# Split weight halves of two FFNs: two separate buffer rings, or one fixed turn of seven over both

## The chip, the cores and the metric

The kernel runs on one core of a Trainium2 chip. The metric is the device time of one execution in microseconds (us), a median over several runs; a lower time is better. A profile of one execution says which engine did what at which time of its span. The engines named here are PE (matrix multiplication), ACT (ScalarE), DVE (VectorE), POOL (GpSimd) and SP (which issues most of the DMAs).

## The reference, cut to what matters

One layer of an encoder is computed for 256 rows of width 2048, in 32-bit floats. The change touches the two half-FFNs, the first and the third stage of the layer:

```python
D_MODEL = 2048
SEQ = 256
D_FF = ((8 * D_MODEL // 3 + 255) // 256) * 256       # 5632

def swiglu(h, w_gate, w_up, w_down):
    return (jax.nn.silu(h @ w_gate) * (h @ w_up)) @ w_down

for i in range(DEPTH):                                # DEPTH = 1
    x = x + 0.5 * swiglu(rms_norm(x, ffn1_norm[i]), ffn1_w_gate[i], ffn1_w_up[i], ffn1_w_down[i])
    ...   # input projection, S5 state-space heads, stick-breaking attention, output projection
    x = x + 0.5 * swiglu(rms_norm(x, ffn2_norm[i]), ffn2_w_gate[i], ffn2_w_up[i], ffn2_w_down[i])
    ...   # per-layer embedding
```

## The kernel before, in words

**Split operands.** Each matrix product is built from rounded parts. A weight tile, 128 x 1024 in 32-bit floats (two blocks of 512 columns), is split into an upper part `hi`, a rounded copy that ACT makes (line 181), and a lower part `lo = src - hi`, which DVE makes (line 184). The activations are split in the same way. PE then adds up three products: hi x hi, lo x hi (both read the weight's upper part) and hi x lo (which reads its lower part). A pair of tiles, one `hi` and one `lo`, is called a half here, since a loaded weight tile `raw` of 128 x 4 x 512 (1 MB) gives two of them.

**Columns and chunks.** The up and gate products of an FFN run over eleven blocks f of 512 columns, the down products over two pairs of such blocks. Part of each block is computed in the plain way: `Seven.column` loads a `raw`, and each of its halves feeds twelve matmuls of 512 columns (`gemm_half`, lines 305, 306 and 310). The rest is computed by `Seven.chunk`, a scheme of the Strassen kind: from two `raw` tiles it forms seven products instead of eight. Three of the seven take a half of a `raw` as it is (products 1, 2, 3), four take a sum of such halves, which DVE adds first (`Seven.add`, line 487; products 5, 6, 4, 7). Each product splits its operand and feeds six matmuls (lines 480, 481, 483). The sums form a chain: t1 feeds product 5, t2 = t1 + ... product 6, t4 = t2 + ... product 4; t3 stands by itself.

**Where chunks are used.** FFN 1 computes its blocks f = 0 to 6 in the plain way, since a preparation for the S5 stage occupies the storage (`early = 7`). At f = 7 that preparation is closed, a pool `sums1` is opened in its storage, DVE forms the sums of activations (`whole_rows`, line 426, and `sum_forms`, line 441), and the chunks begin. FFN 2 has its pool `sums2` from its beginning. At the end of each block f, DVE adds the last product bank (line 606), multiplies (line 608) and turns blocks (`turn_blocks`, line 216).

**The two rings.** A plain half takes its two tiles from the pool `wp` under the tags `whi` and `wlo`, four buffers each. A summed half takes them from the pool of the phase under the tags `shi` and `slo`, three buffers each:

```python
hi, lo = (
    (self.pool if own else wp).tile([P, 2, NB], F32R, tag=s, name=uid(s), bufs=3 if own else None)
    for s in (("shi", "slo") if own else ("whi", "wlo"))
)
```

A half can be split as soon as its ring has a free buffer, that is, when PE has done with the half that used it. The tag `raw` has five buffers, each given back when DVE has done with both halves of it. In the down products two of the five hold x.

**What sets the order.** The program is recorded line by line; a scheduler then orders each engine's instructions before the run, by the recorded order and by when it reckons that operands and buffers are there. On the chip each engine takes its instructions in that order. `step()` runs side work (turns, transfers, norms) that has been put off by so many halves.

Of the kernel before, what the change touches and what calls it, by code (L numbers as in the profile page):

```python
# [2 lines left out]

# [7 lines left out]
F32R = mybir.dt.float32r  # L11
# [5 lines left out]
P = 128  # L17
# [9 lines left out]
NB = 512  # L27
# [6 lines left out]
def layer_kernel(ctx: ExitStack, tc: tile.TileContext, a: dict, shapes: dict, out: bass.AP):  # L34
# [18 lines left out]
    wp = ctx.enter_context(tc.tile_pool(name="wts", bufs=4))  # L53
# [9 lines left out]
    def uid(s):  # L63
        count[0] += 1
        return f"{s}_{count[0]}"
# [7 lines left out]
    def phase(name):  # L73
        return tc.tile_pool(name=name, bufs=1, reuse_waits="tile")
# [175 lines left out]
    def first_quarters(w, xn):  # L250
# [28 lines left out]
        xn.parted(1, second.rearrange("p (j s) -> p j s", j=4))  # L279
        return [(h, *parts[h]) for h in range(2)], weight_split(raws[1], 4)  # L280

    def weight_split(raw, nk, own=None):
        for h in range(nk // 2):
            if own:
                hi, lo = (own.tile([P, 2, NB], F32R, name=uid(s)) for s in ("whi", "wlo"))
            else:
                hi, lo = (wp.tile([P, 2, NB], F32R, tag=s, name=uid(s)) for s in ("whi", "wlo"))
            split(hi, lo, raw[:, 2 * h : 2 * h + 2, :])
            yield h, hi, lo

# [155 lines left out]
    class Seven:  # L446
# [20 lines left out]
            self.begun.add(z)  # L467
            return fresh

        def product(self, z, left, src, own, final):  # L470
            hi, lo = (
                (self.pool if own else wp).tile([P, 2, NB], F32R, tag=s, name=uid(s), bufs=3 if own else None)
                for s in (("shi", "slo") if own else ("whi", "wlo"))
            )
            split(hi, lo, src)
            ps = self.bank(z)
            begin = self.begin(z)
            lh, ll = left
            for j in range(2):
                nc.tensor.matmul(ps, lhsT=lh[j], rhs=hi[:, j], start=begin and j == 0, stop=False)  # L480
                nc.tensor.matmul(ps, lhsT=ll[j], rhs=hi[:, j], start=False, stop=False)  # L481
            for j in range(2):
                nc.tensor.matmul(ps, lhsT=lh[j], rhs=lo[:, j], start=False, stop=z in final and j == 1)  # L483
# [6 lines left out]
        def chunk(self, kb, final=()):  # L490

            raws = []
            for w, n0 in self.ws:
                raw = wp.tile([P, 4, NB], F32, tag="raw", name=uid("raw"), bufs=5)
                nc.sync.dma_start(
                    raw, w[4 * kb * P : 4 * (kb + 1) * P, n0 : n0 + NB].rearrange("(j p) n -> p j n", p=P)
                )
                raws.append(raw)
            b11, b21, b12, b22 = (raw[:, 2 * h : 2 * h + 2, :] for raw in raws for h in range(2))
            parts, sums = self.act(kb), self.sums(kb)  # L500

            def whole(k, t):
                return [[u[:, 2 * k + j, t * P : (t + 1) * P] for j in range(2)] for u in parts]

            def summed(z):
                return [[u[:, z, j * P : (j + 1) * P] for j in range(2)] for u in sums]

            self.product(1, whole(0, 0), b11, False, final)
            t1 = self.add(b11, b12)
            self.product(5, summed(0), t1, True, final)  # L510
            step()
            t2 = self.add(t1, b22)
            self.product(6, summed(1), t2, True, final)
            t4 = self.add(t2, b21)
            self.product(4, whole(1, 1), t4, True, final)
            step()
            t3 = self.add(b12, b22)
            self.product(7, summed(2), t3, True, final)
            self.product(2, whole(1, 0), b21, False, final)
            step()  # L520
            self.product(3, summed(3), b22, False, final)
            step()

        def column(self, side, kbs, final=False):
# [14 lines left out]
    def ffn(i, xn, nxt, bg=None):  # L539
        wg, wu, wd = (a[f"ffn{i}_w_{s}"][0] for s in ("gate", "up", "down"))  # L540
        hT = []
        pools = ExitStack()
        early = 7 if bg else 0
        sevens = None if bg else pools.enter_context(phase(f"sums{i}"))
        hp = pools.enter_context(phase(f"h{i}"))
        side = ExitStack()
        prep = bg(side) if bg else None
# [15 lines left out]
        for f in range(NF):  # L563
            if prep and f == early:
                finish(prep)
                side.close()
                prep = None
                sevens = pools.enter_context(phase(f"sums{i}"))
                hp = pools.enter_context(phase(f"h{i}b"))
                sums = [sum_forms(sevens, whole_rows(sevens, xn(kb)), "h") for kb in range(2)]  # L570
            if sevens and f:
                sg, hh = com("sg"), com("h")
                gate_cols, up_cols = ([u[:, t * NB : (t + 1) * NB] for t in range(TT)] for u in (sg, hh))

                def opened(s, g=gate_cols, u=up_cols):
                    nc.scalar.copy(g[0], s.bank(1))
                    nc.vector.tensor_tensor(out=u[0], in0=s.bank(6), in1=g[0], op=ALU.add)
                    nc.vector.tensor_tensor(out=u[1], in0=s.bank(7), in1=u[0], op=ALU.add)

                def gated(s, g=gate_cols, u=up_cols, hh=hh):  # L580
                    for z, (ps, other) in enumerate(((s.bank(2), g[0]), (s.bank(4), u[1]))):
                        nc.vector.tensor_tensor(out=g[z], in0=ps, in1=other, op=ALU.add)
                        nc.scalar.activation(g[z], g[z], AF.Silu, scale=xn.rs(z))
                    v = hh.rearrange("p (t n) -> p t n", t=TT)
                    nc.vector.tensor_tensor(
                        out=v, in0=s.bank(5).unsqueeze(1).to_broadcast([P, TT, NB]), in1=v, op=ALU.subtract
                    )

                s = Seven(xn, lambda kb: sums[kb], ((wg, f * NB), (wu, f * NB)), sevens)
                two = f % 2 == (0 if bg else 1)  # L590
                if f == early:
                    s.column(0, (1, 2, 3))
                    s.chunk(0, (*shared, 2, 4))
                    put_off(0, opened, s)
                elif two:
                    s.chunk(0)
                    s.column(0, (2, 3))
                    s.chunk(1, (*shared, 2, 4))
                    put_off(0, opened, s)
                else:  # L600
                    s.chunk(0, shared)
                    put_off(0, opened, s)
                    s.column(0, (1, 2, 3), True)
                put_off(0, gated, s)
                s.column(1, (2, 3) if two and f != early else (1, 2, 3), True)
                nc.vector.tensor_tensor(out=hh, in0=s.banks[3.8], in1=hh, op=ALU.add)
                for t in range(TT):
                    nc.vector.scalar_tensor_tensor(
                        out=up_cols[t], in0=up_cols[t], scalar=xn.rs(t), in1=gate_cols[t], op0=ALU.mult, op1=ALU.mult
                    )  # L610
                put_off(2, turned, hp, f, hh)
                continue

            def gate():
                for t in range(TT):
                    nc.scalar.activation(sg[:, t * NB : (t + 1) * NB], pg[t], AF.Silu, scale=xn.rs(t))

            first = ()
            if f == 0 and bg:
                warm_up(10)  # L620
                first = first_quarters(wg, xn)
            if f == 0 and not bg:
                both = gemm_pair(xn, ((wg, 0), (wu, 0)), KD)
                pg = next(both)
                sums = [sum_forms(sevens, whole_rows(sevens, xn(kb))) for kb in range(2)]
            else:
                pg = gemm_block(xn, wg, f * NB, KD, first)
            sg = com("sg")
            if f == 0 and bg:
                for n in range(ND):  # L630
                    put_off(n, load_x, n)
                    put_off(n + 2, xn.squares, n)
                put_off(6, gate)
            else:
                gate()
            pu = gemm_block(xn, wu, f * NB, KD) if f or bg else next(both)
            if prep and f == 0:
                start(prep)
            hh = com("h")
            for t in range(TT):  # L640
                nc.vector.scalar_tensor_tensor(
                    out=hh[:, t * NB : (t + 1) * NB], in0=pu[t], scalar=xn.rs(t),
                    in1=sg[:, t * NB : (t + 1) * NB], op0=ALU.mult, op1=ALU.mult,
                )
            put_off(2, turned, hp, f, hh)
# [31 lines left out]
        for n in range(0, ND, 2):  # L677
# [16 lines left out]
            left = sum(u[0] == "s" for u in plan)  # L694
            for u in plan:
                kb, final = int(u[1:]), u == plan[-1]
# [965 lines left out]
```

## Time and profile before

| | us |
|---|---|
| median of 3 runs | 1852.45 |
| lowest and highest of them | 1851.65 and 1853.28 |
| time of the profiled execution | 1852.7 |
| its span, from the first to the last instruction | 1850.6 |
| PE busy in the span | 1838.3 |
| DVE busy | 1460.6 |
| ACT busy | 1027.4 |

The time of the profiled execution is 2.1 us more than its span; what lies around the span belongs to the start and the end of an execution. Lines such as L184 are lines of the kernel before. In the profile a group of instructions is named by its output and inputs, without buffer numbers: `wlo<-raw,whi` is the lower part of a plain half, `slo<-sum,shi` that of a summed one. In the trace of the changed kernel a plain half may be called `shi` and a summed one `whi`.

### The profile page before, as it was taken

What the parts mean: (1) busy time and instruction counts of PE and PEld (TensorE: products, weight loads), DVE (VectorE), ACT (ScalarE), POOL (GpSimd) and SP (SyncE); (2) the same over time, 40 slices, a digit from 0 to 9 for tenths busy, and PEclk for the clock granted to TensorE, in tenths of its full rate; (3) what the DMA queues carried; (4) which work ended last, traced back from release to release, by engine and by line L of the source; (5) the groups of instructions that cost most, each with busy time, mean ns of one, the idle gap of its engine ahead of it and who ended that gap; (6) DMA issues with size and microseconds to landing.
All of it is one profiled execution on the core that took longest, in us unless ns stands there. A gap on an engine that the chain in (4) does not pass through costs nothing.

```text
span 1850.6 us, 23946 instructions
## 1 busy us (share of the span) xinstructions
PE 1838.3 (99%) x9032; PEld 1518.5 (82%) x9032; DVE 1460.6 (79%) x1718; ACT 1027.4 (56%) x1187; POOL 63.3 (3%) x108
## 2 busy tenths in 40 slices
PE   9999999999999999999999999999999999999998
PEld 7888888778888888888897888888888888888887
DVE  8967665998888876687567798989898978887665
ACT  7444443655564656365685565655555555565654
POOL 0011000000000000010021000000000000000000
PEclk9999999999999999999999999999999999999999
DMA  9888868566756567675646776665656675666663
GB/s 334 281 274 277 252 217 246 173 228 200 241 196 213 192 217 248 190 262 166 216 142 218 224 262 216 235 206 198 218 198 219 207 244 185 223 195 217 208 219 125
DMA packets 232307, 406.36 MB, mean 220 GB/s; under 512 B 26784, under 2 KB 50720, under 8 KB 231904
## 3 DMA queue, kind: packets, MB, share of 16 engines
q1 hardware_dynamic: 227824, 392.81, 63.8%
q0 software_dynamic: 3648, 10.62, 1.8%
q8 instruction: 70, 1.15, 0.2%
q10 hardware_dynamic: 720, 1.41, 0.2%
q14 instruction: 45, 0.37, 0.1%
HBM read 373.46 MB, written 11.93 MB: 208 GB/s over the span
## 4 chain that ended last, share of the span: by engine, by line
PE 92%; DVE 3%; DMA 2%; ACT 2%; SPq 1%; issue 1%; DVEq 0%; ACTq 0%
PE acc L305 18%; PE acc L310 18%; PE acc L306 18%; PE aux L305 7%; PE aux L306 7%; PE aux L310 7%; PE acc L480 3%; PE acc L481 2%; PE acc L483 2%; PE aux L480 2%; PE aux L483 2%; PE aux L481 2%; DVE wlo L184 1%; SPq L1170 1%; DMA raw<-in_w_in 1%
## 5 line engine op out<-in xcount | busy, mean ns | idle before, releaser
L181 ACT CAST whi<-raw 128x1024 fp32r<-128x1024 f32 x639 | 668.1, 1052 | 684.8 <-PE acc L306 388.9
L184 DVE TENSOR_TENSOR wlo<-raw,whi 128x1024 fp32r<-128x1024 f32 x639 | 772.0, 1221 | 297.9 <-ACT whi L181 295.1
L305 PE MATMUL acc<-whi,nhi 128*128 128x512 f32 x1232 | 482.9, 392 | 1.8 <-ACT whi L181 1.7
L306 PE MATMUL acc<-whi,nlo 128*128 128x512 f32 x1232 | 479.9, 390 | 0.0
L310 PE MATMUL acc<-wlo,nhi 128*128 128x512 f32 x1232 | 340.6, 389 | 0.2 <-DVE wlo L184 0.2
L305 PEld LDWEIGHTS acc<-whi,nhi 128*128 128x128 f32 x1232 | 231.5, 188 | 52.2 <-ACT whi L181 3.0
L310 PEld LDWEIGHTS acc<-wlo,nhi 128*128 128x128 f32 x1232 | 231.2, 188 | 48.8 <-DVE wlo L184 0.6
L306 PEld LDWEIGHTS acc<-whi,nlo 128*128 128x128 f32 x1232 | 231.6, 188 | 47.2
L306 PE MATMUL acc<-whi,hlo 128*128 128x512 f32 x376 | 146.4, 389 | 0.0
L305 PE MATMUL acc<-whi,hhi 128*128 128x512 f32 x376 | 146.3, 389 | 0.0
L181 ACT CAST shi<-sum 128x1024 fp32r<-128x1024 f32 x108 | 113.4, 1052 | 43.1 <-DVE sum L487 39.6
L306 PE MATMUL aux<-whi,hlo 128*128 128x512 f32 x344 | 133.8, 389 | 0.0
L305 PE MATMUL aux<-whi,hhi 128*128 128x512 f32 x344 | 133.8, 389 | 0.0
L184 DVE TENSOR_TENSOR slo<-sum,shi 128x1024 fp32r<-128x1024 f32 x108 | 130.9, 1216 | 0.6 <-ACT shi L181 0.5
L310 PE MATMUL acc<-wlo,hhi 128*128 128x512 f32 x376 | 114.6, 389 | 0.2 <-DVE wlo L184 0.2
L310 PE MATMUL aux<-wlo,hhi 128*128 128x512 f32 x344 | 106.0, 389 | 0.0
L306 PE MATMUL aux<-whi,nlo 128*128 128x512 f32 x240 | 93.4, 389 | 0.0
L305 PE MATMUL aux<-whi,nhi 128*128 128x512 f32 x240 | 93.4, 389 | 0.0
L306 PEld LDWEIGHTS acc<-whi,hlo 128*128 128x128 f32 x376 | 70.6, 188 | 15.1 <-DVE hlo L184 0.4
L310 PEld LDWEIGHTS acc<-wlo,hhi 128*128 128x128 f32 x376 | 70.5, 188 | 15.2 <-DVE wlo L184 0.6
L305 PEld LDWEIGHTS acc<-whi,hhi 128*128 128x128 f32 x376 | 70.6, 188 | 14.6
L306 PEld LDWEIGHTS aux<-whi,hlo 128*128 128x128 f32 x344 | 64.6, 188 | 13.5
(345 smaller groups left out, 2162.6 us busy)
## 6 DMA issues: line engine op xcount, KB each, us to landing
raw<-in_ffn_w_up SPq DMA_DIRECT2D x88, 1024.0 KB, 5.8
raw<-in_ffn_w_down SPq DMA_DIRECT2D x88, 1024.0 KB, 5.1
raw<-in_ffn_w_gate SPq DMA_DIRECT2D x86, 1024.0 KB, 6.2
raw<-in_w_in SPq DMA_DIRECT2D x32, 1024.0 KB, 5.7
raw<-in_w_out SPq DMA_DIRECT2D x16, 1024.0 KB, 5.3
raw<-in_w_ple_gate SPq DMA_DIRECT2D x16, 1024.0 KB, 5.1
hT<-mid SPq DMA_DIRECT2D x160, 64.0 KB, 3.5
h<-mid SPq DMA_DIRECT2D x176, 32.0 KB, 3.6
```

Of the source, the lines that this page charges most:

```text
L181: copy = nc.scalar.copy(hi, src)
L184: nc.vector.tensor_tensor(out=lo, in0=src, in1=hi.bitcast(F32), op=ALU.subtract)
L305: nc.tensor.matmul(ps[t], lhsT=lh, rhs=hi[:, j, cols], start=start and j == 0, stop=False)
L306: nc.tensor.matmul(ps[t], lhsT=ll, rhs=hi[:, j, cols], start=False, stop=False)
L310: nc.tensor.matmul(ps[t], lhsT=lh, rhs=lo[:, j, cols], start=False, stop=stop and j == 1)
L480: nc.tensor.matmul(ps, lhsT=lh[j], rhs=hi[:, j], start=begin and j == 0, stop=False)
L481: nc.tensor.matmul(ps, lhsT=ll[j], rhs=hi[:, j], start=False, stop=False)
L483: nc.tensor.matmul(ps, lhsT=lh[j], rhs=lo[:, j], start=False, stop=z in final and j == 1)
L1170: nc.sync.dma_start(zt[0][p1 : p1 + HC, z], sv[p0 : p0 + HC, r % 2 * 2 + r // 2])
```

## The change

The change gives each half of an FFN with chunks, plain or summed, its buffers by one counter. While a pool of sums is open, the halves are numbered i = 0, 1, 2, ... in the order in which the program is recorded; those with i modulo 7 equal to 1, 3 or 5 take `shi` and `slo` of the pool of sums, the other four take `whi` and `wlo` of `wp`. The number of buffers stays four and three. Outside of these phases all halves take `wp`, as before. The tiles' contents and the matmuls are the same. `Seven.product` no longer has an argument `own`.

```diff
+    ring = [None, 0]
+
+    def weight_pair():
+
+        extra, i = ring
+        ring[1] += 1
+        pool, tags = (extra, ("shi", "slo")) if extra and i % 7 % 2 else (wp, ("whi", "wlo"))
+        return [
+            pool.tile([P, 2, NB], F32R, tag=s, name=uid(s), bufs=3 if pool is extra else None) for s in tags
+        ]
+
+    @contextmanager
+    def sums_phase(name):
+        with phase(name) as pool:
+            ring[:] = [pool, 0]
+            yield pool
+            ring[0] = None
+
     def weight_split(raw, nk, own=None):
         for h in range(nk // 2):
             if own:
                 hi, lo = (own.tile([P, 2, NB], F32R, name=uid(s)) for s in ("whi", "wlo"))
             else:
-                hi, lo = (wp.tile([P, 2, NB], F32R, tag=s, name=uid(s)) for s in ("whi", "wlo"))
+                hi, lo = weight_pair()
             split(hi, lo, raw[:, 2 * h : 2 * h + 2, :])
             yield h, hi, lo
...
-        def product(self, z, left, src, own, final):
-            hi, lo = (
-                (self.pool if own else wp).tile([P, 2, NB], F32R, tag=s, name=uid(s), bufs=3 if own else None)
-                for s in (("shi", "slo") if own else ("whi", "wlo"))
-            )
+        def product(self, z, left, src, final):
+            hi, lo = weight_pair()
             split(hi, lo, src)
...
-            self.product(1, whole(0, 0), b11, False, final)
+            self.product(1, whole(0, 0), b11, final)
             t1 = self.add(b11, b12)
-            self.product(5, summed(0), t1, True, final)
+            self.product(5, summed(0), t1, final)
             step()
...
-        sevens = None if bg else pools.enter_context(phase(f"sums{i}"))
+        sevens = None if bg else pools.enter_context(sums_phase(f"sums{i}"))
...
-                sevens = pools.enter_context(phase(f"sums{i}"))
+                sevens = pools.enter_context(sums_phase(f"sums{i}"))
```

The scheduler orders the changed program anew. On PE the order stays that of the products as they are recorded, with some matmuls of neighbouring products exchanged; on ACT and DVE, the two engines that split, many halves move by a few places against each other, and a few loads move on SP. POOL's order is the same.

More of the change, by code (lines that the diff above doesn't have):

```diff
@@ L1 @@
 import math
-from contextlib import ExitStack
+from contextlib import ExitStack, contextmanager
 import concourse.bass as bass
@@ L506, in summed @@
                 return [[u[:, z, j * P : (j + 1) * P] for j in range(2)] for u in sums]
-            self.product(1, whole(0, 0), b11, False, final)
+            self.product(1, whole(0, 0), b11, final)
             t1 = self.add(b11, b12)
-            self.product(5, summed(0), t1, True, final)
+            self.product(5, summed(0), t1, final)
             step()
             t2 = self.add(t1, b22)
-            self.product(6, summed(1), t2, True, final)
+            self.product(6, summed(1), t2, final)
             t4 = self.add(t2, b21)
-            self.product(4, whole(1, 1), t4, True, final)
+            self.product(4, whole(1, 1), t4, final)
             step()
             t3 = self.add(b12, b22)
-            self.product(7, summed(2), t3, True, final)
-            self.product(2, whole(1, 0), b21, False, final)
+            self.product(7, summed(2), t3, final)
+            self.product(2, whole(1, 0), b21, final)
             step()
-            self.product(3, summed(3), b22, False, final)
+            self.product(3, summed(3), b22, final)
             step()
```

## The prediction

> **What bounds the kernel now.** I read the page first, then the stretches of the span by engine, then PE's waits, and last the timelines of PE and DVE where PE waits.
>
> ```profile
> span 1850.6 us, 23946 instructions
> PE 1838.3 (99%) x9032; PEld 1518.5 (82%) x9032; DVE 1460.6 (79%) x1718; ACT 1027.4 (56%) x1187; POOL 63.3 (3%) x108
> ```
>
> PE is the bound: 12.3 us of the span are not PE's. The change leaves every matmul as it is, so all that it can give or take are idle times of PE in the FFN stages. The stretches show where these are (PE, PEld, DVE, ACT, POOL busy with counts, then granted clock, DMA share, GB/s):
>
> ```profile
> 376.00:420.00 44.00, 42.33 (x185) 34.47 (x184) 43.07 (x43) 25.97 (x27) 0.00 (x0) 1.00 0.71 234
> 420.00:600.00 180.00, 180.00 (x793) 148.70 (x792) 152.38 (x152) 100.22 (x102) 4.40 (x8) 1.00 0.63 212
> 1090.00:1380.00 290.00, 290.00 (x1276) 239.03 (x1274) 265.04 (x257) 160.73 (x166) 0.00 (x0) 1.00 0.65 214
> ```
>
> From 420 to 600 us (FFN 1) and from 1090 to 1380 us (FFN 2) PE never idles. There the change can only lose. In the first chunks of FFN 1 DVE is full (43.07 of 44 us) and PE loses. The waits say to whom:
>
> ```profile
> ACT whi L181 <- PE acc L306: 388.9, 272, 3.0
> PE acc L480 <- ACT shi L181: 2.6, 2, 1.7
> PE aux L480 <- ACT shi L181: 0.9, 1, 0.9
> PE acc L310 <- DVE wlo L184: 0.3, 2, 0.2
> ```
>
> The first row is the ring's price to ACT: 388.9 us of waiting for a buffer that PE still reads. It costs PE nothing, since PE's own waits for halves are 2.6, 0.9 and 0.3 us, and they name summed halves or a lower part. The places, with the steady pace ahead of them:
>
> ```profile
> 319.69 0.39 PE L306 MATMUL acc<-whi,nlo 128*128 128x512 f32 x1
> 319.92 0.61 PE L310 MATMUL acc<-wlo,nhi 128*128 128x512 f32 x2
> ...
> 337.80 0.50 PE L480 MATMUL aux<-shi,hhi 128*128 128x512 f32 x1 [0.89 <-ACT shi L181]
> 338.15 0.39 PE L481 MATMUL aux<-shi,hlo 128*128 128x512 f32 x1
> ...
> 366.04 0.50 PE L480 MATMUL acc<-shi,nhi 128*128 128x512 f32 x1 [0.97 <-ACT shi L181]
> ...
> 409.56 0.50 PE L480 MATMUL acc<-shi,nhi 128*128 128x512 f32 x1 [1.67 <-ACT shi L181]
> ...
> 632.72 0.40 PE L481 MATMUL aux<-shi,nlo 128*128 128x512 f32 x1
> 633.26 0.50 PE L483 MATMUL aux<-slo,nhi 128*128 128x512 f32 x1
> ...
> 648.44 0.40 PE L306 MATMUL acc<-whi,hlo 128*128 128x512 f32 x1
> 649.01 0.50 PE L310 MATMUL acc<-wlo,hhi 128*128 128x512 f32 x1 [0.18 <-DVE wlo L184]
> ```
>
> A matmul follows the one before it after 0.23 us (319.69 to 319.92) and lasts 0.39 us, so a wait costs its idle time, plus 0.16 us of overlap, plus 0.12 us (337.80 to 338.15 is 0.35, not 0.23). The three waits of FFN 1's chunks lose 1.17, 1.25 and 1.95 us. In the down products 633.26 comes 0.31 us late and 649.01 0.34 us; with 0.12 each that is 0.43 and 0.46. All five: 5.26 us, the most that the change can win but for crumbs.
>
> **Why PE waits there.** DVE takes its queue in order. Ahead of 366.04:
>
> ```profile
> 360.10 1.22 DVE L606 TENSOR_TENSOR h<-aux,h 128x1024 f32<-128x1024 f32 x1
> 361.23 1.21 DVE L184 TENSOR_TENSOR slo<-sum,shi 128x1024 fp32r<-128x1024 f32 x1
> 362.36 1.41 DVE L608 SCALAR_TENSOR_TENSOR h<-h,sm,sg 128x512 f32<-128x512 f32 x2
> 363.69 1.22 DVE L487 TENSOR_TENSOR sum<-sum,raw 128x1024 f32<-128x1024 f32 x1
> ```
>
> The sum for product 4 ends at 364.91, ACT needs 1.05 us for its upper part, and PE starts at 366.04. It stands behind L606 and L608; ahead of them DVE has already made the plain lower part of product 2, which PE uses after product 4. The plain ring was free and the summed one was not, so the order let the later half go first. With one turn, halves get buffers as they are recorded, and sums and their halves go earlier. On the changed order of instructions I walked each stretch with the durations of these rows.
>
> **Part 1, where the turn begins (f = 7): a new wait.** The second half of the first column now takes `shi`/`slo`, which lie in the storage of the closed preparation. The order after therefore has this half's lower part further back on DVE, as if it had to wait for the storage's last reader, the transfer of `m`:
>
> ```profile
> scr_m<-m SPq DMA_DIRECT2D x1, 1024.0 KB, 6.4
> ```
> ```profile
> 302.84 0.35 SPq L1000 DMA_DIRECT2D scr_m<-m  x1
> 311.24 1.22 DVE L184 TENSOR_TENSOR wlo<-raw,whi 128x1024 fp32r<-128x1024 f32 x1 [1.50 <-ACT whi L181]
> 316.27 1.41 DVE L641 SCALAR_TENSOR_TENSOR h<-acc,sm,sg 128x512 f32<-128x512 f32 x2 [3.81 <-PE acc L310]
> 317.59 1.30 DVE L216 STREAM_TRANSPOSE mid<-h 128x512 f32<-128x512 f32 x2
> 318.81 2.32 DVE L184 TENSOR_TENSOR wlo<-raw,whi 128x1024 fp32r<-128x1024 f32 x2
> 321.05 1.22 DVE L426 TENSOR_TENSOR whole<-nhi,nlo 128x1024 f32<-128x1024 f32 x1
> ```
>
> Before, it is the row at 311.24, and DVE then idles 3.81 us until PE lets L641 go at 316.27. After, it stands behind L641 x2 (to 317.59), L216 x2 (to 318.81), one lower part and L426 (1.13 each start to start: 1.22 less the overlap, as 360.10 to 361.23), so from 321.07 to 322.29. PE wants it at 319.92, the first L310 of that half. Loss: 2.37 us, 0.07 for the release (364.91 plus 1.05 to 366.04), 0.12: 2.56 us. Queued behind it on DVE are the chunk's sums; PE waits for them next. The bounds are 0 (made as at 311.24) and 3.69 (one more DVE step ahead); I take 2.56, since the order on DVE is fixed before the run. The transfer itself, issued at 302.84, lands 6.4 us later at 309.2 and holds nobody. The rest of this chunk begins with DVE one step (1.13 us) late. A chunk asks DVE for eleven steps, 12.4 us, and PE for 42 matmuls, 9.6 us, so no lead is made up; the walk gives waits of 0.38 and 1.10 us, with 0.12 each 1.72, where before there is 1.17. Bounds 0 and 2.30. Part 1 is +2.56 +0.55 = **+3.1 us**.
>
> **Part 2, the next chunks of FFN 1.** At f = 8 the sums now precede products 2 and 3 on DVE: the wait at 366.04 goes, **-1.25** (bounds -1.25 and 0). At f = 9 the wait at 409.56 shrinks, as one plain lower part becomes late in its place by 0.6 us: 0.72 for 1.95, **-1.2** (-1.95 and 0). After that the order matches the sums' needs and PE runs on as in the row 420 to 600.
>
> **Part 3, FFN 1's down products.** Here DVE is fed late:
>
> ```profile
> 619.50 1.23 DVE L487 TENSOR_TENSOR sum<-raw,raw 128x1024 f32<-128x1024 f32 x1 [0.65 <-DMA raw<-in_ffn_w_down]
> ```
>
> Halves that go in recorded order release their `raw` earlier, so SP issues the loads behind them earlier; I keep 0.2 of the 0.89 us: **-0.7** (bounds -0.9, and +1.2 if a DVE step of 1.13 falls the wrong way).
>
> **Part 4, column ends of FFN 2.** Another face of the same order: what goes ahead early leaves less done when DVE stops for PE at L606. One end of before:
>
> ```profile
> 1464.55 1.22 DVE L606 TENSOR_TENSOR h<-aux,h 128x1024 f32<-128x1024 f32 x1 [0.51 <-PE aux L310]
> 1465.69 1.22 DVE L184 TENSOR_TENSOR slo<-sum,shi 128x1024 fp32r<-128x1024 f32 x1
> 1466.82 1.41 DVE L608 SCALAR_TENSOR_TENSOR h<-h,sm,sg 128x512 f32<-128x512 f32 x2
> 1468.14 1.22 DVE L487 TENSOR_TENSOR sum<-raw 128x1024 f32<-128x1024 f32 x1
> ```
> ```profile
> 1469.39 0.62 PE L483 MATMUL acc<-slo,hhi 128*128 128x512 f32 x2
> ...
> 1470.56 0.50 PE L480 MATMUL aux<-shi,nhi 128*128 128x512 f32 x1
> 1470.90 0.39 PE L481 MATMUL aux<-shi,nlo 128*128 128x512 f32 x1
> ```
>
> The lower part at 1465.69 is used by PE at 1469.39. After, a sum (1.13) and both L608 (1.32 each) stand ahead of it: start 1469.46, done 1470.68, 1.29 us late. PE has matmuls of the next product to put in between, so I take 0.75. Two more ends change likewise, by 0.66 and 0.15 in the walk; other ends keep a lead. Before, this end loses 0.11 (1470.56 to 1470.90, less 0.23), and FFN 2 has one more such crumb: 0.2 in all. **+1.35** (bounds: -0.2, and 6.5 if all ten ends lose half of 1.29).
>
> POOL's order is the same and SP's moved loads land ahead of need: 0. If that cover fails, the price is a wait like DVE's 0.65.
>
> **Sum:** 3.1 - 1.25 - 1.2 - 0.7 + 1.35 = +1.3 us. The profiled execution took 1852.7 us, 2.1 beyond its span and 0.25 above the median: 1854.0 by it, 1853.7 against the median of 1852.45. The measurement can tell about 0.2% (3.7 us) from no change, and this is below it.
>
> [...] Row: the stretch 376 to 420 holds an idle time of 1.67 us at a granted clock of 1.00. [...]
>
> **Rivals.**
>
> *Slower: DVE stops at every column end (0.25).* Against the walk, all ten ends of FFN 2 lose. It decides when fewer than four products' lower parts are done as DVE reaches L606: from 1464.55 to the end of the second lower part behind it are about 7.2 us (two lower parts, one sum, 2 x L608, 2 x L216 at the durations above), which PE covers with four products of six matmuls (4 x 1.37), a fifth whose lower part comes first behind L606, and four matmuls of the next. With three, PE waits 0.5 to 0.9 us. For it: DVE is 265 of 290 us busy. Against it: no idle time of PE in that stretch before. Price: ten ends at 0.65 is 6.5, in place of part 4: 1852.45 - 0.05 + 6.3 = 1858.7.
>
> *Faster: no new wait at f = 7 (0.10).* If the lower part is placed ahead of L641, in the 3.81 us that DVE idles, and the sums come early everywhere, all five waits and the crumbs go: -5.26 - 0.2, 1847.0. For it: the storage is free before 316. Against it: the fixed order of DVE. [...]
>
> *Nothing (0.08).* If the ring is never what holds a half, times stay: 1852.45.
>
> **How the numbers follow.** The forecast has 0.57, with 1849 to 1856 from the bounds of its parts, not all at one end. Within 0.2%: forecast and nothing, 0.65. The range goes from 1849.0 to 1859.0, to hold the slower case; the faster one and its neighbours are left out.
>
> **What would show it.** Part 1: an idle time of about 2.4 us on PE at 319.9, its releaser DVE's lower part (L184). Part 2: no wait near 366, and under 0.8 us near 410. Part 3: nothing near 633 and 649. Part 4: small waits at three ends of FFN 2, none over 1.4 us. Wrong would be: DVE's lower part still at 311 and no gap at 320; or waits of 0.5 us at most of FFN 2's ends; or a granted clock below 1.00 after 320.

## The result, and the profile after

The changed kernel takes 1866.07 us (median of 5 runs, 1865.83 to 1866.79); the kernel before took 1852.05 us in the same comparison. The ratio is 1.0075, with a 95% interval of 1.0064 to 1.0086: slower by about 14 us, where 1853.7 was forecast and 1859.0 was the upper end. The page of the changed kernel has these first lines:

```profile
span 1864.2 us, 23966 instructions
PE 1851.6 (99%) x9032; PEld 1517.1 (81%) x9032; DVE 1463.7 (79%) x1718; ACT 1020.3 (55%) x1187; POOL 62.1 (3%) x108
```

The span is 13.6 us longer, PE is busy 13.3 us longer, and PE still has 12.6 us that are not its own (12.3 before). So the time did not go into waiting. PE's waits by what ended them:

```profile
PE acc L328 <- DVE slo L184: 2.2, 1, 2.2
PE acc L323 <- ACT whi L181: 1.8, 3, 1.1
PE aux L248 <- POOL ones L125: 1.1, 1, 1.1
PE aux L495 <- ACT shi L181: 1.0, 1, 1.0
PE acc L323 <- ACT whi L273: 0.7, 1, 0.7
PE acc L328 <- DVE wlo L184: 0.5, 3, 0.2
PE aux L495 <- ACT whi L181: 0.3, 1, 0.3
```

(L323, L324 and L328 are the plain matmuls 305, 306 and 310 of before; L495, L496 and L498 are 480, 481 and 483.) The list adds up to 7.6 us, that of before to 6.6; the 0.7 us from L273 lies at 7.1 us, ahead of everything that the change touches. The stretches shown for before, now in the changed kernel:

```profile
376.00:420.00 44.00, 43.84 (x191) 35.29 (x190) 42.14 (x43) 26.61 (x29) 0.00 (x0) 1.00 0.68 231
420.00:600.00 180.00, 180.00 (x783) 146.76 (x782) 155.40 (x154) 98.92 (x101) 4.39 (x8) 1.00 0.66 223
1090.00:1380.00 290.00, 290.00 (x1261) 236.25 (x1260) 260.62 (x251) 159.29 (x166) 0.00 (x0) 1.00 0.61 208
```

The second and third rows hold the answer in their first bracket. PE is busy for all of the 290 us, at a granted clock of 1.00, and does 1261 matmuls there, where the kernel before does 1276. From 420 to 600 it is 783 for 793. The work is the same, but each matmul takes longer: 290 us over the count is 230.0 ns for 227.3 ns. PE's timeline in the changed kernel, a half in `whi` and `wlo`, the next half in `whi`, then one in `shi`:

```profile
1115.68 0.40 PE L495 MATMUL acc<-whi,hhi 128*128 128x512 f32 x1
1115.91 0.39 PE L496 MATMUL acc<-whi,hlo 128*128 128x512 f32 x1
1116.14 0.40 PE L495 MATMUL acc<-whi,hhi 128*128 128x512 f32 x1
1116.38 0.40 PE L496 MATMUL acc<-whi,hlo 128*128 128x512 f32 x1
1116.61 0.62 PE L498 MATMUL acc<-wlo,hhi 128*128 128x512 f32 x2
1117.07 0.40 PE L495 MATMUL acc<-whi,nhi 128*128 128x512 f32 x1
...
1118.45 0.40 PE L495 MATMUL aux<-shi,nhi 128*128 128x512 f32 x1
1118.69 0.40 PE L496 MATMUL aux<-shi,nlo 128*128 128x512 f32 x1
```

Six matmuls from 1115.68 to 1117.07 are 1.39 us, where six at the steady pace are 1.36. No row has a bracket, so no engine is waited for. To add this up I took all neighbouring pairs of 512-column matmuls whose starts lie less than 0.26 us apart, and counted what each has over 226.7 ns, its excess of pace: 4.5 us in the trace of before, 18.3 us in that of after, **+13.7 us**, nearly all of it in the FFNs (3.4 us there before, 17.0 after). The larger gaps between such matmuls, the waits, add up to 13.0 and 13.7 us: **+0.7 us**, of which 0.6 lies in the first 30 us of the execution. The pace of the matmuls is nearly the whole loss.

That view existed before the change. In the kernel before, PE's groups with shapes kept apart, from 1100 to 1380 us, are (count, then busy time and mean ns of one):

```profile
L306 PE MATMUL acc<-whi,nlo 128*128 128x512 f32 x112 | 43.6, 389 | 0.0
L480 PE MATMUL acc<-whi,hhi 128*128 128x512 f32 x40 | 15.7, 393 | 0.0
L480 PE MATMUL aux<-shi,nhi 128*128 128x512 f32 x40 | 15.7, 393 | 0.0
```

The products of the chunks (L480) were slower than the plain blocks (L306) already, those in `shi` and those in `whi` alike. There were few of them, and the halves in `shi` stood together. That `whi` is slow in the chunks too is taken up under e9 and e10.

### The profile page after: what moved, and what is told of

Read it like the earlier page. It is cut to its first block, busy times and chain, and to the rows that moved or that the text cites. A ratio compares the mean times of both kernels' runs of the same rounds, so it can differ in the third digit from the quotient of the medians.

```text
span 1864.2 us, 23966 instructions
## 1 busy us (share of the span) xinstructions
PE 1851.6 (99%) x9032; PEld 1517.1 (81%) x9032; DVE 1463.7 (79%) x1718; ACT 1020.3 (55%) x1187; POOL 62.1 (3%) x108
## 5 line engine op out<-in xcount | busy, mean ns | idle before, releaser
L184 DVE TENSOR_TENSOR wlo<-raw,whi 128x1024 fp32r<-128x1024 f32 x473 | 573.0, 1223 | 216.0 <-ACT whi L181 207.3
L181 ACT CAST whi<-raw 128x1024 fp32r<-128x1024 f32 x473 | 491.7, 1051 | 406.6 <-PE acc L324 261.7
L323 PE MATMUL acc<-whi,nhi 128*128 128x512 f32 x1112 | 436.7, 393 | 2.6 <-ACT whi L181 1.8
L324 PE MATMUL acc<-whi,nlo 128*128 128x512 f32 x1112 | 433.5, 390 | 0.0
L328 PE MATMUL acc<-wlo,nhi 128*128 128x512 f32 x1112 | 304.3, 389 | 0.3 <-DVE wlo L184 0.3
L323 PEld LDWEIGHTS acc<-whi,nhi 128*128 128x128 f32 x1112 | 208.7, 188 | 49.1 <-ACT whi L181 3.2
L328 PEld LDWEIGHTS acc<-wlo,nhi 128*128 128x128 f32 x1112 | 208.6, 188 | 45.3 <-DVE wlo L184 1.2
L324 PEld LDWEIGHTS acc<-whi,nlo 128*128 128x128 f32 x1112 | 208.8, 188 | 43.1 <-DVE nlo L274 0.3
L184 DVE TENSOR_TENSOR slo<-raw,shi 128x1024 fp32r<-128x1024 f32 x166 | 202.3, 1219 | 45.8 <-ACT shi L181 45.6
L181 ACT CAST shi<-raw 128x1024 fp32r<-128x1024 f32 x166 | 173.7, 1047 | 117.4 <-PE acc L324 34.6
L181 ACT CAST whi<-sum 128x1024 fp32r<-128x1024 f32 x61 | 64.0, 1050 | 97.2 <-DVE sum L502 83.5
L181 ACT CAST shi<-sum 128x1024 fp32r<-128x1024 f32 x47 | 49.4, 1051 | 73.6 <-DVE sum L502 65.7
L323 PE MATMUL acc<-whi,hhi 128*128 128x512 f32 x216 | 85.2, 395 | 0.0
L324 PE MATMUL acc<-whi,hlo 128*128 128x512 f32 x216 | 84.6, 392 | 0.0
L323 PE MATMUL aux<-whi,hhi 128*128 128x512 f32 x200 | 78.9, 395 | 0.0
L324 PE MATMUL aux<-whi,hlo 128*128 128x512 f32 x200 | 78.4, 392 | 0.0
L184 DVE TENSOR_TENSOR wlo<-sum,whi 128x1024 fp32r<-128x1024 f32 x61 | 74.6, 1223 | 2.1 <-ACT whi L181 1.4
L184 DVE TENSOR_TENSOR hlo<-hT,hhi 128x1024 fp32r<-128x1024 f32 x56 | 68.2, 1218 | 6.7 <-ACT hhi L181 6.5
L181 ACT CAST hhi<-hT 128x1024 fp32r<-128x1024 f32 x56 | 58.5, 1044 | 16.2 <-PE aux L328 13.6
L502 DVE TENSOR_TENSOR sum<-sum,raw 128x1024 f32<-128x1024 f32 x54 | 66.0, 1222 | 1.0
L328 PE MATMUL acc<-wlo,hhi 128*128 128x512 f32 x216 | 65.7, 390 | 0.2 <-DVE wlo L184 0.2
L323 PE MATMUL acc<-shi,hhi 128*128 128x512 f32 x160 | 63.1, 394 | 0.0
```

What stands on the lines that cost most here:

```text
L181: copy = nc.scalar.copy(hi, src)
L184: nc.vector.tensor_tensor(out=lo, in0=src, in1=hi.bitcast(F32), op=ALU.subtract)
L323: nc.tensor.matmul(ps[t], lhsT=lh, rhs=hi[:, j, cols], start=start and j == 0, stop=False)
L324: nc.tensor.matmul(ps[t], lhsT=ll, rhs=hi[:, j, cols], start=False, stop=False)
L328: nc.tensor.matmul(ps[t], lhsT=lh, rhs=lo[:, j, cols], start=False, stop=stop and j == 1)
L502: nc.vector.tensor_tensor(out=t, in0=x, in1=y, op=ALU.add)
```

## The experiments

**What differs between the rings.** The tiles' places in a partition's storage are fixed when the kernel is compiled. All four `whi` and four `wlo` buffers start at the same offset within 256 bytes, and so do the activations' split tiles. These are the stationary operands of PE's matmuls (`lhsT`, 128 x 128, the LDWEIGHTS rows of the profile); the weight halves are the streamed ones (`rhs`, 128 x 512). The pool of sums lies behind a pool of ten small tiles of 32 bytes each and has another offset. The experiments move whole pools by pads of a few bytes. To have room, `rho4` (128 bytes) is kept in a part of `gains` that is no longer needed. Except in e8 and e11, the instructions of every engine stand in the order of the kernel from which they were made. The table has the offsets of the compiled programs and the median times; e8 and e11 have e4's offsets.

```
offset within 256 B   whi/wlo  activations  shi/slo    us
before                  160       160         224    1852.05
after                   160       160         224    1866.07
e1 (after)               32        32         160    1864.76
e2 (before)              32        32         160    1853.24
e3 (after)               96        96         160    1865.85
e4 (after)              128       128         128    1849.65
e5 (after)              128       128         192    1866.88
e6 (after)               32        32          32    1850.32
e7 (before)             128       128         128    1849.38
e9 (after)               32        96          32    1896.85
e10 (after)              32        96          96    1887.52
```

**e1: the extra ring moved by 64 bytes.**

```diff
+            pool.tile([P, 16], F32, tag="pad", name=uid("pad"), bufs=1)
             ring[:] = [pool, 0]
...
-    rho4 = cpool.tile([P, NR], F32, name="rho4")
+    rho4 = gains[:, NCOL : NCOL + NR]
```

> The changed kernel with the extra ring's tiles moved by 64 bytes (a pad at the head of the pool of sums; 128 bytes of room come from keeping rho4 in a free part of the tile gains). Offsets within 128 bytes: whi/wlo stay at 32, shi/slo go from 96 to 32; the order on every engine is that of the changed kernel. Theory A (a matmul's pace depends on the byte offset at which its streamed operand begins, and on a change of that offset from one half to the next): the trace of the changed kernel has matmul starts 13.7 us further apart in sum than before, beside waits that are only 0.7 us longer; of its 17.0 us of excess over 226.7 ns in the FFNs all but 1 to 2 us goes, so 1866.1 - 15 to 16 = about 1850 to 1851. Rival H (what matters is the height of the storage, above 150 KB, or the change between two regions as such): it stays 1866. Rival S (the loss is in waits for split halves): 1866, with the same waits.

Measured: 1864.76 us, ratio 1.0066 (1.0053 to 1.0078). Theory A, with its 128 bytes, is wrong: the two rings now agree within 128 bytes and the loss is there. Its excess of pace is 16.6 us. Within 256 bytes the rings are still 128 apart.

**e2: the same in the kernel before.**

```diff
         sevens = None if bg else pools.enter_context(phase(f"sums{i}"))
+        if sevens:
+            sevens.tile([P, 16], F32, tag="pad", name=uid("pad"), bufs=1)
...
                 sevens = pools.enter_context(phase(f"sums{i}"))
+                sevens.tile([P, 16], F32, tag="pad", name=uid("pad"), bufs=1)
```

> The kernel before with the same 64-byte move of shi/slo and rho4 kept in gains; order on every engine as before. Theory A: the excess over 226.7 ns in its FFNs is 3.4 us (1.2, 0.15, 1.9, 0.2 by stage) and goes: about 1849.0. Rivals H and S: 1852.0, no change.

Measured: 1853.24 us, ratio 1.0004 (0.9995 to 1.0013). No gain either, as e1 now lets one expect; the excess went from 4.5 to 5.8 us.

**e3: everything behind the constants moved by 64 bytes**, so that the offsets within 128 bytes change places.

```diff
+    cpool.tile([P, 16], F32, name="pad")
-    rho4 = cpool.tile([P, NR], F32, name="rho4")
+    rho4 = gains[:, NCOL : NCOL + NR]
```

> The changed kernel with everything behind the constants moved so that the classes are exchanged: whi/wlo and the activations at 96 within 128 bytes, shi/slo at 32. Order as in the changed kernel. Theory A in its absolute form (offset 96 is the slow one: 229 ns a matmul in long rows, offset 32 226.7): most of 7,500 matmuls at 96 cost 2.3 ns each, some +13 us more than the changed kernel's plain halves, changes between halves cost as now: 1875 to 1885. In its relative form (only the change between halves, or a difference to the stationary operand, costs): 1866, as the changed kernel. Rival H: 1866.

Measured: 1865.85 us, ratio 1.0073 (1.0059 to 1.0086), as the changed kernel. Neither of the two offsets is slow in itself; only how operands stand to each other can matter, or the storage's height.

**e4: all at 0 within 128 bytes.**

```diff
-    smp = ctx.enter_context(tc.tile_pool(name="small", bufs=10))
+    smp = ctx.enter_context(tc.tile_pool(name="small", bufs=8))
...
+    cpool.tile([P, 24], F32, name="pad")
-    rho4 = cpool.tile([P, NR], F32, name="rho4")
+    rho4 = gains[:, NCOL : NCOL + NR]
```

> The changed kernel with all tiles of the rings and of the activations at 0 within 128 bytes (pad in front, rho4 kept in gains, the ring of small tiles cut from ten to eight). Order as in the changed kernel. Theory A: one class for all, so the changes between halves are gone: 1850 or less. If a row of 2048 bytes that begins off a boundary of 128 bytes costs one more piece (17 for 16), the steady 226.7 ns would fall to 213 and the time by up to 9,000 x 13 ns = 120 us, until DVE's 1464 us and the waits set the end: 1735 to 1790. Rivals H and S: 1866.

Measured: 1849.65 us, ratio 0.9986 (0.9977 to 0.9995): 16 us less than the changed kernel, and a little faster than the kernel before. The storage's height changed by under 200 bytes, and neither the order nor the alternation of the rings changed, so rivals H and S fall. The furthest part of the expectation, a pace of 213 ns, did not come: the steady pace stayed at 226.7 ns. The stretch 1100 to 1380 in before, after and e4:

```profile
1100.00:1380.00 280.00, 280.00 (x1232) 230.87 (x1230) 255.04 (x247) 156.37 (x162) 0.00 (x0) 1.00 0.65 214
```
```profile
1100.00:1380.00 280.00, 280.00 (x1217) 228.11 (x1216) 251.93 (x242) 151.59 (x157) 0.00 (x0) 1.00 0.63 214
```
```profile
1100.00:1380.00 280.00, 280.00 (x1237) 231.82 (x1236) 255.70 (x246) 152.59 (x159) 0.00 (x0) 1.00 0.63 213
```

PE is full in all three, and does 1232, 1217 and 1237 matmuls. By groups e4 has the same 389 ns for both rings:

```profile
L325 PE MATMUL acc<-whi,nlo 128*128 128x512 f32 x62 | 24.1, 389 | 0.0
L324 PE MATMUL aux<-shi,nhi 128*128 128x512 f32 x44 | 17.1, 389 | 0.0
```

e4 left two readings: that all operands stand at multiples of 64 bytes (theory C), or that they have one offset within 256 bytes (theory B).

**e5 and e6: the two readings apart.** e5 is e4 with ten small tiles again, so the rings are at multiples of 64 but 64 bytes apart. e6 has no pad and eight small tiles: all at 32. Against e4:

```diff
-    smp = ctx.enter_context(tc.tile_pool(name="small", bufs=8))      # e5
+    smp = ctx.enter_context(tc.tile_pool(name="small", bufs=10))
...
-    cpool.tile([P, 24], F32, name="pad")                             # e6
```

> The changed kernel with whi/wlo at 0 within 128 bytes (128 within 256) and shi/slo at 64 (192 within 256); order as in the changed kernel. Theory C (a matmul pays when its operands begin off a multiple of 64 bytes and the ring changes): no excess of pace, 1849.6 as with all tiles at 0 within 128. Theory B (the two rings must stand at the same offset within 256 bytes): slow, 1864 to 1866. If multiples of 128 are wanted for all: slow too.

> The changed kernel with all rings and the activations at the same offset within 256 bytes, 32, so off every multiple of 64 (rho4 kept in gains, ten small tiles cut to eight, no pad); order as in the changed kernel. Theory B: 1849.6. Theory C: slow, 1864 to 1866.

Measured: e5 1866.88 us, ratio 1.0075 (1.0062 to 1.0089); e6 1850.32 us, ratio 0.9986 (0.9977 to 0.9995). Theory B holds and C falls. In e4 and e6 the rings differ by 256 bytes within 512, which does no harm (1849.65 and 1850.32 us); in e1 they differ by 128, which does (1864.76 us). So in these runs the distance counts by its remainder within 256 bytes.

**e9 and e10: who has to agree with whom.** In e1 to e6 `whi` and the activations had one offset. Here a pad of 64 bytes stands in the activations' pool, and the small tiles (six in e9, eight in e10) bring `shi` either to `whi`'s offset or to the activations'.

```diff
+    actp.tile([P, 16], F32, name="pad")
```

> The changed kernel with whi/wlo and shi/slo at the same offset within 256 bytes (32) and the activations' split tiles, the stationary operands, at another (96); order as in the changed kernel. Theory B1 (only the change between the two rings of streamed tiles costs): no excess of pace, about 1850. Theory B2 (a streamed tile is slow when its offset differs from the stationary tile's): every matmul of the rings is slow, in the plain blocks f = 0 to 6 too: at the 229 to 233 ns of the long rows of shi some 8,000 x 2.3 to 6 ns = 18 to 50 us more than 1850: 1868 to 1900.

> The changed kernel with shi/slo and the activations' split tiles at the same offset within 256 bytes (96) and whi/wlo at another (32); order as in the changed kernel. Theory B1: the rings differ, so as the changed kernel, 1864 to 1867, and the plain blocks f = 0 to 6 keep 226.7 ns. Theory B2: the plain halves become slow everywhere (all of f = 0 to 6 and the middle stages), the summed ring's halves keep 226.7 ns: 6,000 matmuls x 2.3 to 6 ns = 14 to 36 us more than 1850, 1864 to 1886; told apart by the pace in the plain blocks and in the rows of shi.

Measured: e9 1896.85 us, ratio 1.0239 (1.0222 to 1.0256); e10 1887.52 us, ratio 1.0188 (1.0173 to 1.0203). Theory B2 holds: in these runs the matmuls whose streamed tile and stationary tiles have different offsets within 256 bytes are slow, with means of 230 to 233 ns from start to start for 226.7. (All stationary tiles have one offset, so whether the matmul's own counts, or that of the next one, was not told apart.) In e9 the two rings agree and everything is slow, the plain blocks at the beginning too. Stretch 30 to 120 us, in the changed kernel and in e9:

```profile
30.00:120.00 90.00, 90.00 (x399) 74.53 (x398) 77.89 (x201) 48.65 (x66) 0.34 (x1) 1.00 0.80 265
```
```profile
30.00:120.00 90.00, 90.00 (x387) 72.50 (x387) 76.60 (x199) 47.30 (x65) 0.34 (x1) 1.00 0.80 266
```

In e10 the same stretch has 387 too, and the groups from 1100 to 1380 tell the rings apart, `whi` slow throughout and `shi` in part:

```profile
L325 PE MATMUL acc<-whi,nhi 128*128 128x512 f32 x68 | 26.8, 394 | 0.0
L325 PE MATMUL acc<-shi,nhi 128*128 128x512 f32 x52 | 20.2, 389 | 0.0
L326 PE MATMUL acc<-shi,nlo 128*128 128x512 f32 x52 | 20.4, 393 | 0.0
```

Counted from start to start over the whole trace, `whi` and `wlo` have 233.3 ns; `shi` and `slo` have 230.0 ns in the first six matmuls after a half in `whi`, and 226.7 ns from the seventh on. So the forecast for `shi` came true only there, and e10's time lies 1.5 us above the range that B2 was given.

So a mismatch outlasts itself. In the changed kernel the halves in `whi` agree with the activations, yet those behind a mismatched half are slow as well. In its FFNs, with the turn on, the 2061 counted pairs that begin at a matmul on `shi` or `slo` have a mean of 230.5 ns and 7.8 us of excess; the 1949 that begin within ten matmuls behind one have 231.5 ns and 9.3 us, so more than half of the loss falls on matmuls that agree; the 1202 further away have 226.8 ns. With a distance of 128 bytes (e1) only the first three behind are slow, 231.7 ns, and the next seven have 226.9. The matmuls that read `shi` or `slo` rise from 648 to 2070 in the program; with those behind them, the slow pace covers three quarters of the FFN matmuls in the turn.

**e7: the kernel before with e4's offsets.** The edit is e4's, made in the kernel before. It tells what the turn of seven does once the offsets are out of the way.

> The kernel before, moved as the changed kernel was in the run with all tiles at 0 within 128 bytes; its own order on every engine. Its trace has 3.4 us of matmul starts too far apart in the FFNs: if these go as they did in the changed kernel, 1852.4 - 3.4 = 1849.0, and the turn of seven alone, by its waits, is worth 1849.65 - 1849.0 = +0.6 us (the prediction's sum was +1.3, the difference of waits in the two traces 0.7). Rival: the move does nothing to a kernel that changes rings rarely: 1852.4, and then the turn of seven is worth -2.7 us by itself.

Measured: 1849.38 us, ratio 0.9983 (0.9974 to 0.9992). Its excess of pace is 1.0 us, so its 3.5 us went as expected. Against e4's ratio of 0.9986 the turn of seven alone is worth +0.0003, some +0.5 us, with intervals of about 0.0009 to each side: no difference that could be told. In the traces the waits of the two FFNs add up to 5.7 us in e4 and 5.5 in e7, and e4 has 1.6 us besides at half clock (0.57 granted from 323 to 327 us) behind the gap at 320 us (last section).

**e8: the first two halves at f = 7 take `wp`** (on e4).

```diff
-    def sums_phase(name):
+    def sums_phase(name, first=0):
         with phase(name) as pool:
-            ring[:] = [pool, 0]
+            ring[:] = [pool, first]
...
-                sevens = pools.enter_context(sums_phase(f"sums{i}"))
+                sevens = pools.enter_context(sums_phase(f"sums{i}", 6))
```

> The changed kernel with all tiles at 0 within 128 bytes, its turn begun at 6 in FFN 1, so that the first two halves at f = 7 take wp and the third is the first to take shi/slo. On DVE the lower part that PE wanted at 319.9 stands ahead of L641 again, and the next half's stands where it stood. By the step called part 1: the wait of 2.38 us at 319.9 goes, the next half's lower part is then up to 0.5 us late: 1849.65 - 1.9 to 2.5 = 1847.2 to 1847.8. Rival (the lost time only moves to the chunk, where DVE is as late as before): 1849.6.

Measured: 1848.72 us, ratio 0.9977 (0.9968 to 0.9985), 0.9 us below e4 by the medians, 0.0009 by the ratios. The wait at 320 us is gone, and most of it comes back in the chunk behind it, as the waits of e8 show:

```profile
337.50 0.50 PE L496 MATMUL aux<-whi,hhi 128*128 128x512 f32 x1 [1.38 <-ACT whi L182]
...
342.29 0.50 PE L499 MATMUL acc<-slo,nhi 128*128 128x512 f32 x1 [0.52 <-DVE slo L185]
...
345.70 0.50 PE L499 MATMUL aux<-wlo,hhi 128*128 128x512 f32 x1 [0.35 <-DVE wlo L185]
```

From 315 to 420 us, e4 loses 5.0 us in its trace: 3.4 in waits, and 1.6 by a stretch at half clock (0.57 granted from 323 to 327 us) behind the gap, shown in the last section, which also delays PE so that the next wait isn't met. e8 loses 4.0 us there, all in waits. So the rival was nearly right: the wait moves into the chunk and the waits grow by 0.6 us, but e8 has no stretch at half clock (behind its longest wait the starts are 0.23 us apart again, 337.83 to 338.06). What is left of the gain is 1.0 us there, and 0.8 us by the spans (1847.7 and 1846.9). The intervals of the two ratios overlap; the times alone don't tell them apart.

**e11: e8 with two separate rings again in FFN 2.**

```diff
-    def weight_pair():
+    def weight_pair(own=False):
         extra, i = ring
-        ring[1] += 1
-        pool, tags = (extra, ("shi", "slo")) if extra and i % 7 % 2 else (wp, ("whi", "wlo"))
+        if i is not None:
+            ring[1] += 1
+            own = i % 7 % 2
+        pool, tags = (extra, ("shi", "slo")) if extra and own else (wp, ("whi", "wlo"))
...
-            hi, lo = weight_pair()
+            hi, lo = weight_pair(z in (4, 5, 6, 7))
...
-        sevens = None if bg else pools.enter_context(sums_phase(f"sums{i}"))
+        sevens = None if bg else pools.enter_context(sums_phase(f"sums{i}", None))
```

> The run with all tiles at 0 within 128 bytes and the turn begun at 6 in FFN 1 (1848.72, ratio 0.9977), with FFN 2 back to two separate rings (shi/slo for products 5, 6, 4, 7); the order from FFN 2 on is that of before. By the step called part 4 the turn of seven adds waits at column ends of FFN 2 (1.39 us there against 0.23 in the kernel before): 1.1 us less, ratio 0.9971, about 1847.6 on the same footing. Rival (the waits at those ends come with the aligned tiles or are hidden otherwise): ratio 0.9977.

Measured: 1847.79 us, ratio 0.9975 (0.9966 to 0.9985). In the trace FFN 2's waits fall from 1.35 us in e8 to 0.41, as part 4 has it; the ratio moved by 0.0002 where 0.0006 was expected, which these runs cannot tell from either. It is the fastest kernel of the study by its median, 4.6 us below the kernel before in its own comparison (1852.35 us).

## Why the prediction was wrong

**The step that failed** stands in its first part: "The change leaves every matmul as it is, so all that it can give or take are idle times of PE in the FFN stages." Every matmul is the same instruction on the same numbers, but its streamed operand lies elsewhere, and PE's pace depended on that here: 226.7 ns when the two operands agreed within 256 bytes, and means of 230 to 233 ns when they didn't and for up to ten matmuls behind. The prediction read its pace from one pair of starts on a `whi` half (319.69 to 319.92) and used it for all. This left a term of +13.7 us out of the sum, and no rival held it. All rivals were waits, and the slower one (DVE at every column end of FFN 2) did not occur either.

**The steps on waits held.**

- Part 1 forecast a loss of 2.56 us at 319.9 with DVE's lower part as the releaser. After:

```profile
319.87 0.40 PE L324 MATMUL acc<-shi,nlo 128*128 128x512 f32 x1
322.48 0.72 PE L328 MATMUL acc<-slo,nhi 128*128 128x512 f32 x2 [2.21 <-DVE slo L184]
```
```profile
316.42 1.41 DVE L656 SCALAR_TENSOR_TENSOR h<-acc,sm,sg 128x512 f32<-128x512 f32 x2 [6.53 <-PE acc L328]
317.75 1.29 DVE L216 STREAM_TRANSPOSE mid<-h 128x512 f32<-128x512 f32 x2
318.97 1.19 DVE L184 TENSOR_TENSOR wlo<-raw,whi 128x1024 fp32r<-128x1024 f32 x1
320.07 1.21 DVE L444 TENSOR_TENSOR whole<-nhi,nlo 128x1024 f32<-128x1024 f32 x1
321.21 1.22 DVE L184 TENSOR_TENSOR slo<-raw,shi 128x1024 fp32r<-128x1024 f32 x1
```

  The start is 2.61 us after the one before it, 2.38 us late, and with 0.11 for the next one the loss is 2.49 us. DVE runs the five steps in the forecast order, ending at 322.43 where 322.29 was forecast. The rest of the chunk was put at 1.72 us and lost 1.47, so part 1 is +2.8 us for +3.1:

```profile
342.98 0.51 PE L495 MATMUL aux<-shi,hhi 128*128 128x512 f32 x1 [0.97 <-ACT shi L181]
```

- Part 2: no wait near 366, as forecast (-1.25). Near 410 the forecast was 0.72 us, measured 0.43 plus a crumb of 0.08, so -1.4 for -1.2:

```profile
415.88 0.62 PE L498 MATMUL aux<-slo,hhi 128*128 128x512 f32 x2
416.66 0.73 PE L328 MATMUL acc<-wlo,nhi 128*128 128x512 f32 x2 [0.16 <-DVE wlo L184]
```

- Part 3: nothing is left in FFN 1's down products but 0.08 us; 0.2 was kept (-0.8 for -0.7).
- Part 4: three ends of FFN 2 wait, as said, and none over 1.4 us. They lose 0.57, 0.07 and 0.51 us, 1.16 in all, so +0.9 for the forecast +1.35:

```profile
1396.76 0.50 PE L495 MATMUL aux<-whi,nhi 128*128 128x512 f32 x1 [0.30 <-ACT whi L181]
...
1486.23 0.73 PE L328 MATMUL acc<-wlo,hhi 128*128 128x512 f32 x2 [0.16 <-DVE wlo L184]
```

By these places the waits came to +0.2 us for +1.3 forecast, each part being as its term or a little better. With all crumbs, the waits of both FFNs add up to 5.8 us in either trace; the +0.7 us of the whole trace lies in the first 30 us (0.6) and between the FFNs. e4 against e7, where the pace is the same in both kernels, gives +0.0003 of the time. So the mechanism that the prediction walked through is right and small, and another one, which it had excluded, set the result.

**The buffers and the clock.** With the pace equal, seven buffers in one turn bring nothing that can be told (e4 and e7, +0.0003). A granted clock below 1.00 after 320 was named as a sign that the prediction is wrong: in the profiled run of the changed kernel it stays at 1.00 from 323 to 327 us, behind the new gap, but in those of e4 and e6 it is 0.57 and 0.59 (last section).

## What to carry to other kernels

When a change moves a matmul's operand to other storage, compare PE's starts for each operand tile, not for one of them, and count matmuls in stretches where PE is full: here a lower count at full clock (1261 for 1276 in 290 us at 1.00) was a loss that no view of waits showed. By e4 to e10 it paid here to keep the streamed and the stationary tiles of these 32-bit matmuls at the same offset within 256 bytes; the pool of ten small tiles of 32 bytes between them broke this, and a pad of a few bytes or another number of small tiles mended it (-16 us on the changed kernel, -3 on the kernel before).

## What the hardware showed that was not expected

**Offsets.** In these runs the pace of a 128 x 512 matmul depends on the distance of its two operands within 256 bytes. With equal offsets it is 226.7 ns, at each offset that was tried (32, 96, 128 and 160). With the streamed tile's offset 64 bytes above the stationary one's (before, e3, e5) long rows run at 229 ns, with the first four at 231 to 236; with 128 bytes (e1, e2) at 233; with 64 bytes the other way (e9, e10) at 233.3. Which part of the machine makes this was not shown, nor why the two directions differ; distances of less than 64 bytes were not tried.

**The clock after a gap of 2.4 us.** Eight of the kernels have the gap at 320 us (in e9 and e10 at 331): PE starts 2.3 to 2.4 us late, and its rows show 2.1 to 2.2 us of idle time. In e4 and e6 PE runs at half pace shortly after it. In e4:

```profile
322.39 0.73 PE L329 MATMUL acc<-slo,nhi 128*128 128x512 f32 x2 [2.24 <-DVE slo L185]
...
325.00 0.63 PE L324 MATMUL acc<-whi,nhi 128*128 128x512 f32 x1
325.43 0.63 PE L325 MATMUL acc<-whi,nlo 128*128 128x512 f32 x1
325.86 0.63 PE L324 MATMUL acc<-whi,nhi 128*128 128x512 f32 x1
```
```profile
323.00:327.00 4.00, 4.00 (x12) 3.14 (x11) 4.00 (x6) 1.99 (x2) 0.00 (x0) 0.57 0.86 270
```

Seven starts are 0.43 us apart instead of 0.23, which costs 1.4 us (1.6 with the starts at either end), and the granted clock of the stretch is 0.57. In e6 it is 0.59, with 12 matmuls in the same 4 us as well. In the changed kernel itself and in e1 the same gap has no such effect: the granted clock there is 1.00, and PE does 19 matmuls. The idle time is nearly the same, 2.24 us in e4 and 2.21 in the changed kernel; what decides was not shown.
